# Other heaps for the down-projection's 1/rms products and for the copies and sums between seven half products

## The chip, the cores and the metric

The kernel runs on one core of a Trainium2 chip. The metric is the device time of one execution in microseconds (us). The engines of the core are named as the profile names them: PE is TensorE (matmuls), PEld its weight loads, DVE is VectorE, ACT is ScalarE, POOL is GpSimd and SP is SyncE, which issues the DMAs here.

## The reference

The input x has 512 tokens of 1,024 features. Two layers of a first block (a feed-forward network, a mixer of a recurrent scan, dilated attention and a convolution, and a second feed-forward network) are followed by a second block: a gated linear attention (GLA) mixer, a feed-forward network with a three-tap convolution on its gate, a sparse attention mixer (NSA), a second such feed-forward network, and a last RMS norm. What the change touches is the feed-forward network (FFN), six times in all, and the norms ahead of whatever comes behind one:

```python
def _rms_norm(x, g):
    xf = x.astype(jnp.float32)
    y = xf * lax.rsqrt(jnp.mean(xf * xf, axis=-1, keepdims=True) + NORM_EPS)
    return y.astype(x.dtype) * g
...
def _swiglu(x, w_gate, w_up, w_down):
    return (jax.nn.silu(x @ w_gate) * (x @ w_up)) @ w_down
```

The hidden width is 2,816, that is 22 tiles of 128.

## The kernel before

Activations lie feature by feature, 128 features on the partitions and 512 tokens in a row, so x is eight tiles of 128x512. Each float32 matrix is cut into a high part (`hi`, `whi`, by ACT) and a low part (`lo`, `wlo`, by DVE, source minus high part), and a product is three matmuls: high by high, high by low, low by high.

An FFN (`ffn`, L455) first scales x and takes the sums of squares for 1/rms (`norm_r`, L332: squares `nsq` on ACT, their sum `nacc` on POOL, a product with ones into the bank `po`); the factor R = 1/rms is multiplied in behind the products. Then it walks over the 22 hidden tiles in two halves of 11. A tile is made in one of two ways. `eight` makes gate and up by eight k-tiles each, 48 matmuls of 512 columns. `seven` splits the 2x2 product of gate and up weights by token halves in Strassen's manner (Winograd's form): seven products instead of eight, each 12 matmuls of 256 columns, summed in the halves of two PSUM banks X and Y. Products 1 and 2 go to the first half of X, 5 and 3 to the second, 6 and 7 to the first half of Y, 4 to the second. The four plain FFNs have 11 such tiles each (SEVEN, L155: 5, 6, 8, 9, 11, 12, 14, 15, 17, 18, 20, so five pairs of neighbours and a single one), the two with the convolution 8 each (SEVEN_CONV, L156: 5, 7, ... 19). That is 60.

In a `seven` tile, DVE makes sums of the weights (L403, L404 into `ws`; L408 and L410 in place into `raw`), and `cut` (L365 on ACT, L366 on DVE) splits them. The cut of L404's sum is the second half of S (products 5 and 6), the cut of L403's is the first half. L410's result is cut into `wsh` and `wsl` (W, product 3). Between products, ACT copies the halves of X to `wp` (P, L429 behind product 1, L433 behind product 5), and DVE adds: `fv` (L431 behind product 6, L438 behind product 7), `fu` (L439, L440), `fg` (L436, L442, L443). Behind each half of the hidden tiles, the down-projection makes eight output tiles by `gemm` (L280 to L282); L483 multiplies each by R into `fd`, and L484 adds it to x. The last norm is `final` (L1475): squares on ACT (L1481), sums on POOL (L1483), `po` on PE (L1487), `nms` on DVE (L1491).

SBUF tiles of 128x512 come from heaps (HEAPS, L149): a heap is a ring of slots, given out in the order of the program text: n, x, r0 and r1 have 16, aq 7, ap 6, o 3 and rs 3. A new tile of a heap takes the slot of an old one and waits until that one's last reader is through. `ws`, `wp`, `fg`, `fu`, `fv` lie in r0, `wsh` and `wsl` in ap, and `fd` in the default heap, which an FFN sets to o (`self.on("o", "rr")`); the norms' `nacc`, `nsq` and `bex` lie in o as well.

The order of each engine's instructions isn't that of the text: a list scheduler orders them by a modelled timeline and by priorities (`RANK`), and takes the slots' waits into account. So a heap's change can move instructions on every engine.

Of the kernel before, what the change touches and what calls it, by code (L numbers as in the profile page):

```python
# [18 lines left out]
T = 512  # L19
# [171 lines left out]
class Net:  # L191
# [202 lines left out]
    def seven(self, wgu, f, F, R):  # L394


        n, H = T // 2, D // 2
        a, b = slice(0, n), slice(n, T)
        p, q = slice(0, H), slice(H, D)
        rg, ru = [self.raw(wgu[f, :, i * D:(i + 1) * D], D) for i in range(2)]  # L400
        s1, s2 = [self.s([128, H], "ws", heap="r0") for _ in range(2)]
        S, G, U = self.parts(D), self.parts(D), self.parts(D)
        self.V.tensor_tensor(s1, ru[:, p], ru[:, q], OP.add)  # L403
        self.V.tensor_tensor(s2, s1, rg[:, p], OP.subtract)  # L404
        self.cut(rg, *G)
        self.cut(s2, *[t[:, q] for t in S])
        self.cut(s1, *[t[:, p] for t in S])
        self.V.tensor_tensor(ru[:, p], rg[:, p], ru[:, p], OP.subtract)  # L408
        self.cut(ru, *U)
        self.V.tensor_tensor(rg[:, q], rg[:, q], s2, OP.subtract)  # L410
        W = [self.s([128, H], nm, F32R, "ap") for nm in ("wsh", "wsl")]
        self.cut(rg[:, q], *W)
        half = lambda t, c: [y[:, c] for y in t]
        A = {1: half(G, p), 2: half(G, q), 3: W, 4: half(U, q), 5: half(S, p), 6: half(S, q), 7: half(U, p)}
        X, Y = [self.ps([128, T], next(self.banks)) for _ in range(2)]

        def product(i, ps, first=False):
            hi, lo = A[i]
            for j in range(4):
                xh, xl = F[i][j]  # L420
                w = slice(j * 128, (j + 1) * 128)
                self.T.matmul(ps, hi[:, w], xh, start=first and j == 0, stop=False, skip_group_check=True)  # L422
                self.T.matmul(ps, hi[:, w], xl, start=False, stop=False, skip_group_check=True)  # L423
                self.T.matmul(ps, lo[:, w], xh, start=False, stop=j == 3, skip_group_check=True)  # L424

        P, g, u, v = [self.s([128, T], nm, heap="r0") for nm in ("wp", "fg", "fu", "fv")]
        B, E = Y[:, a], Y[:, b]
        product(1, X[:, a], True)
        self.A.activation(P[:, a], X[:, a], AF.Copy)  # L429
        product(6, B, True)  # L430
        self.V.tensor_tensor(v[:, a], B, P[:, a], OP.add)  # L431
        product(5, X[:, b])
        self.A.activation(P[:, b], X[:, b], AF.Copy)  # L433
        product(4, E)
        product(2, X[:, a])
        self.V.tensor_tensor(g[:, a], X[:, a], R[:, a], OP.mult)  # L436
        product(7, B)
        self.V.tensor_tensor(v[:, b], B, P[:, a], OP.add)  # L438
        self.V.tensor_tensor(u[:, a], E, v[:, b], OP.add)  # L439
        self.V.tensor_tensor(u[:, b], v[:, b], P[:, b], OP.add)  # L440
        product(3, X[:, b])
        self.V.tensor_tensor(g[:, b], X[:, b], v[:, a], OP.add)  # L442
        self.V.tensor_tensor(g[:, b], g[:, b], R[:, b], OP.mult)  # L443
        return g, u

    def eight(self, wgu, f, xs, R):
# [5 lines left out]
        return g, pu  # L452

    def ffn(self, x, gname, l, wgu, wdn, scale, seven, conv=None):


        self.on("o", "rr")
        xs = self.scaled(x, gname, KT * l)
        R = self.norm_r(x)
        factors = self.seven_x(x, xs, gname, KT * l)  # L460
        F = next(factors)
        self.banks = cycle(("mm", "rr", "at", "mm", "rx", "at"))
        M = NF // 2
        for part in range(2):
            h = []
            for i in range(M):
                f = part * M + i
                g, u = self.seven(wgu, f, F, R) if f in seven else self.eight(wgu, f, xs, R)
                if conv:
                    g = conv(g, l, f)  # L470
                self.A.activation(g, g, AF.Silu)
                self.V.tensor_tensor(g, u, g, OP.mult)
                h.append(self.split(g, None, HALF[i]))
                if 1 <= f < 5:
                    next(factors)
            for n in range(KT):
                pd = self.ps([128, T], next(self.banks))
                for a, b in ((0, 6), (6, M)):
                    o = part * M
                    w = self.load_w(wdn[n, :, (o + a) * 128:(o + b) * 128], (b - a) * 128)  # L480
                    self.gemm(pd, w, h.__getitem__, a, b, a == 0, b == M)
                y = self.s([128, T], "fd")
                self.V.scalar_tensor_tensor(y, pd, scale, R, OP.mult, OP.mult)  # L483
                self.V.tensor_tensor(x[n], x[n], y, OP.add)  # L484
        self.banks = repeat("mm")
# [1121 lines left out]
```

## Time and profile before

| | us |
|---|---|
| Time, median of 3 runs | 3455.41 |
| Lowest and highest run | 3453.07, 3463.67 |
| Profiled execution, its time | 3454.09 |
| Profiled execution, its span | 3452.3 |
| PE busy | 3381.1 (98%) |
| DVE busy | 2273.9 (66%) |
| ACT busy | 1448.1 (42%) |
| POOL busy | 324.5 (9%) |
| Mean granted clock of TensorE | 0.992 |

The span runs from the first to the last instruction of the profiled execution. Matmuls are pipelined: a row of the timeline gives a matmul's start and duration, and the next starts before it has ended, so the spacing of the starts is what a matmul costs. The idle time in brackets is counted from the end of the one ahead. A granted clock of 1.00 is 2.4 GHz, one of 0.50 is 1.2 GHz.

### The profile page before, as it was taken

How to read it: one execution, taken by the hardware profiler on the slowest of the kernel's cores; microseconds unless marked ns; L12 is line 12 of the kernel's file. 1: busy time of each engine (PE TensorE's matmuls, PEld its weight loads, DVE VectorE, ACT ScalarE, POOL GpSimd, SP SyncE). 2: the span in 40 equal slices, each digit the busy share in tenths (PEclk: the TensorE clock that was granted, in tenths of full speed). 3: DMA queues.
4: the chain of work that ended last, by engine and by line, in shares of the span. 5: the costliest groups of instructions: out<-in, count | busy, mean ns of one | idle time of the engine just before them, and what ended most of it. 6: DMA issues, size and time to landing. Idle time of an engine off the chain costs nothing.

```text
span 3452.3 us, 49155 instructions
## 1 busy us (share of the span) xinstructions
PE 3381.1 (98%) x19286; PEld 2798.2 (81%) x19286; DVE 2273.9 (66%) x3973; ACT 1448.1 (42%) x2390; POOL 324.5 (9%) x377
## 2 busy tenths in 40 slices
PE   8999999999999999999999999999999999999997
PEld 7888777878888889877878888777888887788886
DVE  7566597667575757569766666486766664467573
ACT  5333434354243424343445334344533444654342
POOL 1000116010001000013301000120100010210000
PEclk9999999999999999999999999999999999999998
DMA  4333322132333232423123333321333442132322
GB/s 135 100 102 101 116 81 63 38 128 89 93 98 101 92 94 97 115 94 79 47 87 98 97 94 115 117 71 53 104 88 102 135 121 79 50 113 83 106 88 67
DMA packets 134536, 321.94 MB, mean 93 GB/s; under 512 B 33152, under 2 KB 35744, under 8 KB 134304
## 3 DMA queue, kind: packets, MB, share of 16 engines
q1 hardware_dynamic: 134304, 318.81, 30.3%
q8 instruction: 151, 2.47, 0.3%
q14 instruction: 81, 0.66, 0.1%
HBM read 303.81 MB, written 14.94 MB: 92 GB/s over the span
## 4 chain that ended last, share of the span: by engine, by line
PE 47%; DVE 4%; ACT 1%; issue 0%; POOL 0%; POOLq 0%; DVEq 0%; ACTq 0%
PE mm L280 5%; PE mm L281 5%; PE mm L282 5%; PE at L281 3%; PE at L280 3%; PE at L282 3%; PE rx L281 2%; PE rx L282 2%; PE rx L280 2%; PE rr L281 1%; PE rr L282 1%; PE rr L280 1%; PE mm L422 1%; PE mm L424 1%; PE mm L423 1%; PE at L424 1%
## 5 line engine op out<-in xcount | busy, mean ns | idle before, releaser
L268 ACT ACTIVATE whi<-raw 128x1024 fp32r<-128x1024 f32 (+3 forms) x494 | 444.2, 900 | 899.7 <-PE mm L281 363.3
L269 DVE TENSOR_TENSOR wlo<-raw,whi 128x1024 fp32r<-128x1024 f32 (+3 forms) x494 | 518.4, 1050 | 262.4 <-ACT whi L268 261.4
L280 PE MATMUL mm<-xh,whi 128*128 128x512 f32 x896 | 359.6, 402 | 8.5 <-ACT whi L268 8.4
L282 PE MATMUL mm<-xh,wlo 128*128 128x512 f32 x896 | 361.4, 403 | 0.0
L281 PE MATMUL mm<-xl,whi 128*128 128x512 f32 x896 | 359.7, 401 | 0.0
L341 POOL TENSOR_TENSOR nacc<-nacc,nsq 128x512 f32<-128x512 f32 x70 | 106.4, 1520 | 1994.3 <-ACT nsq L340 1991.5
L280 PEld LDWEIGHTS mm<-xh,whi 128*128 128x128 f32 x896 | 169.9, 190 | 52.8 <-ACT whi L268 8.4
L280 PE MATMUL mm<-hi,whi 128*128 128x512 f32 x520 | 206.0, 397 | 2.5 <-ACT hi L297 1.4
L281 PEld LDWEIGHTS mm<-xl,whi 128*128 128x128 f32 x896 | 169.6, 189 | 44.8 <-issue 6.0
L282 PE MATMUL mm<-hi,wlo 128*128 128x512 f32 x520 | 205.8, 396 | 0.0
L281 PE MATMUL mm<-lo,whi 128*128 128x512 f32 x520 | 205.6, 395 | 0.1
L282 PEld LDWEIGHTS mm<-xh,wlo 128*128 128x128 f32 x896 | 169.5, 189 | 41.4 <-issue 3.2
L281 PE MATMUL at<-xl,whi 128*128 128x512 f32 x496 | 197.2, 398 | 0.0
L282 PE MATMUL at<-xh,wlo 128*128 128x512 f32 x496 | 196.9, 397 | 0.0
L280 PE MATMUL at<-xh,whi 128*128 128x512 f32 x496 | 196.1, 395 | 0.0
L365 ACT ACTIVATE whi<-raw 128x1024 fp32r<-128x1024 f32 x120 | 127.2, 1060 | 147.6 <-PE mm L423 55.5
L366 DVE TENSOR_TENSOR wlo<-raw,whi 128x1024 fp32r<-128x1024 f32 x120 | 146.5, 1221 | 37.9 <-ACT whi L365 37.9
L422 PE MATMUL mm<-xh,whi 128*128 128x256 f32 x552 | 158.2, 287 | 4.3 <-ACT wp L429 4.1
L424 PE MATMUL mm<-xh,wlo 128*128 128x256 f32 x552 | 156.5, 283 | 0.9 <-DVE wlo L366 0.7
L281 PE MATMUL at<-lo,whi 128*128 128x512 f32 x396 | 156.8, 396 | 0.0
L282 PE MATMUL at<-hi,wlo 128*128 128x512 f32 x396 | 156.8, 396 | 0.0
L280 PE MATMUL at<-hi,whi 128*128 128x512 f32 x396 | 155.6, 393 | 0.0
(748 smaller groups left out, 8472.3 us busy)
## 6 DMA issues: line engine op xcount, KB each, us to landing
raw<-ffn_gu SPq DMA_DIRECT2D x176, 512.0 KB
raw<-c_gu SPq DMA_DIRECT2D x88, 512.0 KB
raw<-ffn_dn SPq DMA_DIRECT2D x64, 384.0 KB
raw<-w_in SPq DMA_DIRECT2D x46, 512.0 KB
raw<-ffn_dn SPq DMA_DIRECT2D x64, 320.0 KB
raw<-c_dn SPq DMA_DIRECT2D x32, 384.0 KB
raw<-c_dn SPq DMA_DIRECT2D x32, 320.0 KB
raw<-a_w_in SPq DMA_DIRECT2D x17, 512.0 KB
```

The lines of the kernel that those rows point to most:

```text
L268: self.A.activation(hi, raw, AF.Copy)
L269: self.V.tensor_tensor(lo, raw, hi.bitcast(F32), OP.subtract)
L280: self.T.matmul(ps, wh, xh, start=first and j == 0, stop=False)
L281: self.T.matmul(ps, wh, xl, start=False, stop=False)
L282: self.T.matmul(ps, wl, xh, start=False, stop=last and j == nk - 1)
L341: self.G.tensor_tensor(acc, acc, sq, OP.add)
L365: self.A.activation(hi, src, AF.Copy)
L366: self.V.tensor_tensor(lo, src, hi.bitcast(F32), OP.subtract)
L422: self.T.matmul(ps, hi[:, w], xh, start=first and j == 0, stop=False, skip_group_check=True)
L423: self.T.matmul(ps, hi[:, w], xl, start=False, stop=False, skip_group_check=True)
L424: self.T.matmul(ps, lo[:, w], xh, start=False, stop=j == 3, skip_group_check=True)
```

## The change

Three names move to the heap ap: `wp` and `fv` of `seven` from r0, and `fd` of the down-projection from o. `fg` and `fu` stay in r0. The counts of instructions on each engine stay. The added line moves every line behind L426 by one: L429 becomes L430.

```diff
@@ -423,7 +423,8 @@
-        P, g, u, v = [self.s([128, T], nm, heap="r0") for nm in ("wp", "fg", "fu", "fv")]
+        P, v = [self.s([128, T], nm, heap="ap") for nm in ("wp", "fv")]
+        g, u = [self.s([128, T], nm, heap="r0") for nm in ("fg", "fu")]
...
@@ -479,7 +480,7 @@
-                y = self.s([128, T], "fd")
+                y = self.s([128, T], "fd", heap="ap")
```

The text of one engine's work is moved by the scheduler. ACT in the second tile of a pair of neighbours (the tile at 237 to 252 us of the trace), before; `whi_2149` is S, `whi_2153` U, and `at_2171` and `mm_2172` are the banks X and Y:

```order
L429 ACTIVATE wp_2173<-at_2171 128x256
L365 ACTIVATE whi_2149<-ws_2148 128x512
L365 ACTIVATE whi_2153<-raw_2145 128x1024
L365 ACTIVATE wsh_2167<-raw_2143 128x512
L433 ACTIVATE wp_2173<-at_2171 128x256
L471 ACTIVATE fg_2041<-fg_2041 128x512
```

The same place now:

```order
L365 ACTIVATE whi_2149<-ws_2148 128x512
L365 ACTIVATE whi_2153<-raw_2145 128x1024
L365 ACTIVATE wsh_2167<-raw_2143 128x512
L430 ACTIVATE wp_2173<-at_2171 128x256
L472 ACTIVATE fg_2042<-fg_2042 128x512
```

The first copy to `wp` has moved from ahead of S's second half to behind `wsh`. PE in the same tile, before, from the end of the tile ahead (`wsh_2034`, product 3) on; the next five rows but one belong to products 5 (bank `at_2171`) and 6 (bank `mm_2172`):

```order
L424 MATMUL mm_2038<-xh_148,wsl_2035 128x256
L422 MATMUL at_2171<-xh_341,whi_2149 128x256
L423 MATMUL at_2171<-xl_342,whi_2149 128x256
L422 MATMUL mm_2172<-xh_345,whi_2149 128x256
L423 MATMUL mm_2172<-xl_346,whi_2149 128x256
L424 MATMUL at_2171<-xh_341,wlo_2150 128x256
L422 MATMUL at_2171<-xh_428,whi_2149 128x256
```

The same place now, with the start of product 5 and of product 4 (`whi_2153`) behind the lines left out:

```order
L424 MATMUL mm_2038<-xh_148,wsl_2035 128x256
L422 MATMUL mm_2172<-xh_345,whi_2149 128x256
L423 MATMUL mm_2172<-xl_346,whi_2149 128x256
L424 MATMUL mm_2172<-xh_345,wlo_2150 128x256
L422 MATMUL mm_2172<-xh_432,whi_2149 128x256
...
L424 MATMUL mm_2172<-xh_606,wlo_2150 128x256
L422 MATMUL at_2171<-xh_341,whi_2149 128x256
...
L424 MATMUL at_2171<-xh_602,wlo_2150 128x256
L422 MATMUL mm_2172<-xh_345,whi_2153 128x256
```

Product 6 now runs whole ahead of product 5, and product 4 follows at once. ACT at the end of the program, in the last down-projection, before (`x` is the residual, `vec` holds the norm's weights):

```order
L268 ACTIVATE whi_30762<-raw_30760 128x640
L1481 ACTIVATE nacc_30784<-x_27082 128x512
L1481 ACTIVATE nsq_30788<-x_27084 128x512
L1489 ACTIVATE x_27082<-x_27082,vec 128x512
L1489 ACTIVATE x_27084<-x_27084,vec 128x512
L1481 ACTIVATE nsq_30792<-x_27086 128x512
```

And now:

```order
L268 ACTIVATE whi_30493<-raw_30491 128x768
L1482 ACTIVATE nacc_30784<-x_27082 128x512
L1490 ACTIVATE x_27082<-x_27082,vec 128x512
L268 ACTIVATE whi_30517<-raw_30515 128x640
L268 ACTIVATE whi_30542<-raw_30540 128x768
L1482 ACTIVATE nsq_30788<-x_27084 128x512
L1490 ACTIVATE x_27084<-x_27084,vec 128x512
L268 ACTIVATE whi_30566<-raw_30564 128x640
```

The squares and the scaling of the last norm stood behind the last weight cut (`whi_30762`); now those of the first six tiles of x stand between the cuts, and those of the last two behind them.

## Rows read from the trace of the kernel before

**Rows 1.** The page, busy time of each engine, with its share and instructions:

```profile
PE 3381.1 (98%) x19286; PEld 2798.2 (81%) x19286; DVE 2273.9 (66%) x3973; ACT 1448.1 (42%) x2390; POOL 324.5 (9%) x377
```

**Rows 2.** PE's waits: line waited for, us in total, times, longest us:

```profile
PE po L1487 <- POOL nacc L1483: 9.0, 1, 9.0
PE rx L422 <- ACT wp L429: 5.1, 10, 1.5
```

**Rows 3.** Timeline of DVE, a pair's second tile: start, us, operation, [idle before]:

```profile
239.34 0.43 DVE L436 TENSOR_TENSOR fg<-mm,bR 128x256 f32<-128x256 f32 x1 [1.32 <-PE mm L424]
240.34 0.68 DVE L403 TENSOR_TENSOR ws<-raw 128x512 f32<-128x512 f32 x1
241.06 0.69 DVE L404 TENSOR_TENSOR ws<-ws,raw 128x512 f32<-128x512 f32 x1
243.81 0.68 DVE L366 TENSOR_TENSOR wlo<-ws,whi 128x512 fp32r<-128x512 f32 x1
247.09 0.42 DVE L431 TENSOR_TENSOR fv<-mm,wp 128x256 f32<-128x256 f32 x1
```

**Rows 4.** Timeline of ACT in the same tile:

```profile
241.68 0.37 ACT L429 ACTIVATE wp<-at 128x256 f32<-128x256 f32 x1
241.94 0.62 ACT L365 ACTIVATE whi<-ws 128x512 fp32r<-128x512 f32 x1
243.92 0.63 ACT L365 ACTIVATE wsh<-raw 128x512 fp32r<-128x512 f32 x1 [0.41 <-DVE raw L410]
```

**Rows 5.** Timeline of PE in the same tile:

```profile
242.10 0.38 PE L422 MATMUL at<-xh,whi 128*128 128x256 f32 x1 [0.24 <-ACT wp L429]
245.72 0.28 PE L424 MATMUL mm<-xh,wlo 128*128 128x256 f32 x1
```

**Rows 6.** Timeline, PE and DVE, first pair of the first FFN:

```profile
71.95 0.39 PE L422 MATMUL rx<-xh,whi 128*128 128x256 f32 x1 [0.24 <-ACT wp L429]
72.13 0.68 DVE L366 TENSOR_TENSOR wlo<-ws,whi 128x512 fp32r<-128x512 f32 x1
82.52 0.39 PE L422 MATMUL mm<-xh,whi 128*128 128x256 f32 x1 [0.47 <-ACT wp L429]
```

**Rows 7.** Timeline, PE and DVE, a tile of a convolution FFN:

```profile
2532.35 0.28 PE L424 MATMUL mm<-xh,wlo 128*128 128x256 f32 x1
2532.24 0.69 DVE L366 TENSOR_TENSOR wlo<-ws,whi 128x512 fp32r<-128x512 f32 x1
2536.45 0.42 DVE L431 TENSOR_TENSOR fv<-rr,wp 128x256 f32<-128x256 f32 x1
```

**Rows 8.** Timeline, PE and DVE, first seven-product tile of a convolution FFN:

```profile
2488.89 0.39 PE L422 MATMUL rx<-xh,whi 128*128 128x256 f32 x1 [1.55 <-ACT wp L429]
2490.77 0.68 DVE L366 TENSOR_TENSOR wlo<-ws,whi 128x512 fp32r<-128x512 f32 x1
```

**Rows 9.** Windows, PE: stretch, us, busy (matmuls), granted clock, DMA share, GB/s:

```profile
2489.40:2492.80 3.40, 3.00 (x22) 1.00 0.00 0
3120.40:3123.80 3.40, 3.40 (x17) 0.50 0.06 14
244.40:247.80 3.40, 3.40 (x29) 1.00 0.23 35
```

**Rows 10.** Timeline of ACT, POOL, PE and DVE at the last norm:

```profile
3428.70 1.15 ACT L1481 ACTIVATE nsq<-x 128x512 f32<-128x512 f32 x2 [5.84 <-DVE x L484]
3429.47 6.65 POOL L1483 TENSOR_TENSOR nacc<-nacc,nsq 128x512 f32<-128x512 f32 x5 [6.41 <-ACT nsq L1481]
3437.90 1.84 PE L1487 MATMUL po<-cpack,nsq 128*128 128x1 f32 x8
3439.78 0.16 DVE L1491 TENSOR_SCALAR nms<-po 128x4 f32<-128x4 f32 x1 [11.12 <-PE po L1487]
```

**Rows 11.** Timeline of POOL and PE at the norm ahead of GLA:

```profile
2206.89 11.08 POOL L341 TENSOR_TENSOR nacc<-nacc,nsq 128x512 f32<-128x512 f32 x7 [363.03 <-ACT nsq L340]
2227.03 1.08 PE L324 MATMUL po<-cpack,bex 128*128 128x128 f32 x4 [3.85 <-DVE bex L321]
```

## The prediction

> **What bounds the kernel now.** I read the page's busy times first: TensorE is busy 98% of the span [rows 1], so every microsecond that it doesn't wait is taken, and the time can only move where it waits now or will wait. The profiled execution took 3454.1 us (span 3452.3 and 1.8 around it), which stands in the middle of the runs' 3453.1 to 3463.7, 1.3 under their median; I sum against it. Next I read TensorE's waits: the largest is one of 9.0 us for the sum of squares before the last norm, and the next kinds are short repeated ones of the seven-product tiles for the copy `wp` [rows 2]. Then I read the timelines of VectorE, ScalarE and TensorE in one such tile, the second of a pair at 237 to 252 us, which repeats 16 times [rows 3, 4, 5], and the rows of the other kinds of tile.
>
> In that tile product 1's part ends and the next matmul would start at 241.70 (the row at 242.10 waited 0.24, and matmuls here start 0.16 before the one ahead has ended). It starts at 242.10, when `wp` (241.68 + 0.37 = 242.05) is there; 24 matmuls later the last of products 5 and 6 starts at 245.72 instead of 241.70 + 23 x 0.12 = 244.46 [rows 5]. The tile costs 1.25 us of waiting. The 0.12 us is the spacing at full clock: 29 matmuls in 3.40 us [rows 9]. What holds the tile is VectorE: it works without a gap from 239.34 (waiting for TensorE's product 2) through L440, L403, L404, the cuts, to L431 at 247.09 [rows 3].
>
> **Part 1: `wp` and `fv` in heap ap.** No instruction is added or removed; only orders change. In ap the slots are handed out in program order, and `wsh` and `wsl` stand ahead of `wp` there; ScalarE so writes `wp` behind `wsh` (order excerpt of ScalarE), whose input L410 comes late: `wsh` starts at 243.92 and ends at 244.55 [rows 4], while `wp` was done at 242.05. TensorE's program pays for it: product 5, which needs `wp` read out of its bank, no longer opens with two matmuls beside two of product 6; all twelve of 6 come first, then 5, then 4 at once (order excerpt of TensorE).
>
> *Second tile of a pair, 16 times.* (i) Product 6 needs `whi`'s second half, cut from L404's result (241.06 + 0.69 = 241.75 [rows 3]); with `wp` gone from ahead of it the 0.62 us cut [rows 4] ends near 242.46, so the first matmul starts at 242.51 in place of 241.70: 0.81, and 0.10 for the slow first step that follows each pause (0.22 to the next one, not 0.12). (ii) The third matmul of product 6 needs the second half of `wlo`, which VectorE finishes at 243.81 + 0.68 = 244.49 [rows 3]; VectorE's order is the same up to there in both programs. TensorE would be there at 242.85 and starts at 244.54: 1.69 + 0.10. Before, ten matmuls of product 5 covered this wait. (iii) Product 4 writes the bank that L431 reads, and L431 ends at 247.09 + 0.42 = 247.51 [rows 3]; product 4 is reached 10 + 12 matmuls on, at 247.28, and starts at 247.55: 0.27 + 0.10. Before, product 2 covered it. Sum 3.07 for 1.25: +1.82 x 16 = **+29.1**.
>
> *First pair of the four plain FFNs, 4 times.* First tile: `wp` cost 0.24 + 0.16 + 0.10 = 0.50; now the third matmul of product 6, due at 71.55, waits for the cut that ends at 72.81 [rows 6]: 72.86 - 71.55 = 1.31 + 0.10 = 1.41, +0.91. Second tile: it waits 0.23 longer than the other pairs' at its start (0.47 against 0.24 [rows 5, 6]), so about 1.5, and gets the order above, 3.07: +1.57. Together +2.5 x 4 = **+10**.
>
> *Tiles of the two convolution FFNs.* In ten of them product 1 ends at 2532.35 [rows 7] and the like; the third matmul of 6, due 0.36 later at 2532.71, waits for `wlo` (2532.24 + 0.69 = 2532.93), starts at 2532.98: 0.27 + 0.10. Product 5 follows, and product 4, due at 2535.72, waits for L431 (2536.45 + 0.42 = 2536.87 [rows 7]): 1.20 + 0.10. Less the 0.49 for `wp` that goes, +1.18 in the six tiles of this order; in four tiles two matmuls of 512 columns (0.47) stand between 5 and 4, so +0.71. 6 x 1.18 + 4 x 0.71 = +9.9. The first tile of each FFN waits 1.55 for `wp` and 2.7 in all its pauses now; by [rows 8] product 6's third matmul, due at 2488.89 - 1.55 + 0.08 = 2487.42, starts behind 2490.77 + 0.68 = 2491.45: 4.08 + 0.10, +1.5 each. Together **+12.9**.
>
> **Part 2: `fd` out of heap o.** Heap o has three slots and is then left to the norm's squares and sums; they need not wait behind the last `fd`. At the end, five additions of 6.65 us on GpSimd and 16 small matmuls run after the last sum of x, and `nms` starts at 3439.78 [rows 10]. In the new program the squares of six of the eight tiles stand between the cuts of the last down-projection (order excerpt of ScalarE at the end), and the seventh follows its sum; only the last tile's square is left, starting at 3428.70 (two take 1.15), then 8 matmuls (1.84, or half at full clock [rows 10]): `nms` at 3430.3 to 3431.3, a gain of 8.5 to 9.4; **-9.0**. The norm ahead of the GLA mixer is the same case: seven additions of 11.08 us run after 2206.89, and TensorE waits 3.85 us for the broadcast at 2227.03 [rows 11]: **-3.9**, as a later wait there stays. What hides the squares now is the down-projection, where ScalarE and GpSimd have room; the 7 squares of 0.6 us add to ScalarE before the weight cuts, bounded by 0 and by one square (0.6) for each of 6 FFNs; I take 0. The order in the mixers shifts too; TensorE shows no wait for a norm there, so between -5 and +5, taken as 0.
>
> **The clock.** With these alone: 3454.1 + 29.1 + 10 + 12.9 - 9.0 - 3.9 = 3493. The pause of 1.55 us and the shorter ones behind it at 2488 were followed by a granted clock of 1.00 (2.4 GHz) [rows 8, 9]; the same tile of the second convolution FFN, with the same pauses, was followed from 3120 by 3.4 us at 0.50 (1.2 GHz), 17 matmuls where 29 fit [rows 9], and so was the old 1.25 us of pauses at 242 [rows 9]. A fall costs 12 matmuls of 0.12, about 1.5 us, less the 0.3 of product 4's wait that it swallows: 1.2. The new pauses are 2.6 to 3.1 us, in 20 pairs. One of two cases fell, so I take half: 10 x 1.2 = **+12**. Forecast: 3505 us. By the Trainium skill, TensorE: Matmul & The Clock Gate, section "A second HAM failure mode: psum-queue depth-cycling", an engine that idles briefly between groups of matmuls can swing between its two clocks again and again. The trace agrees at one of the two spots, 0.50 at 3120 and 1.00 at 2489; by the page all pairs would fall, rival B.
>
> **Rivals.** *A: no pair loses the clock.* The stalls come as worked out, 3493 us. For it: 1.00 behind the pauses at 2488; against: 0.50 at 3120.
>
> *B: every pair and both long tiles lose it.* 22 x 1.5 = 33 on 3493: 3526 us. For it: the new pauses together are longer than those that did it once.
>
> *C, the other side: the heap r0 was what held the cuts.* A seven-product tile takes six of r0's 16 slots now and four afterwards. If `ws` (L403) could then start earlier, both halves of `wlo` would be ready when product 6 comes. It decides at L403 about 1.8 us earlier: from there the second tile costs no more than now, and the time is 3454.1 - 12.9 = 3441; with 3 us more, all waits go, 16 x 1.25 + 4 x 2.0 in pairs and 10 x 0.5 + 2 x 2.7 in the convolution FFNs: 28 + 10 more, 3403 us. Against it: L403 starts at 240.34, back to back with the VectorE work ahead of it, which is held by TensorE's product 2 (1.32 us of idle before 239.34), not by a slot [rows 3], and in the new order it stands in the same place. The Trainium skill, Perfetto Trace Analysis, section "Identifying Performance Opportunities", says that a gap that repeats on the engine that should be saturated can mean that memory for the next tile was lacking. That would be this rival and its 3441 or less; the trace disagrees, since the gap's cause is VectorE's queue without idle time.
>
> *D: it moves nothing that counts.* If the stalls grew by only a quarter of my sum, 13 us, the 12.9 of part 2 would eat it: 3454 us. It would need ScalarE's `wp` ahead of L410 after all, which the program's order excludes.
>
> **How the numbers follow.** Forecast with half of the clock losses, 3505: 0.48. A, 3493: 0.22. B, 3526: 0.18. C: 0.06. D: 0.06. The predicted time is 3505. The low end, 3482, takes A with 11 us for the unknowns (mixers 5, one wait of part 1 mis-sized by 0.3 us in 20 pairs); the high end, 3528, takes in B. About 0.3%, 10 us, can be told from no change by a measurement here. Slower by more than that: forecast, A and B, 0.88; the same 0.06 (D); faster 0.06 (C).
>
> **What would show it.** In the changed profile TensorE's waits in the seven-product tiles should be for L366's `wlo` (about 1.6 us, 20 times) and no longer for `wp`; a pair's second tile should show three waits near 0.8, 1.7 and 0.3 us; the row of `wsh` ahead of `wp` on ScalarE; the 9.0 us wait before `po` gone and `nms` under 2 us after the last square; the 3.85 us at the GLA norm gone. The granted clock behind the pairs tells the forecast from A and B: half of them at 0.50. It would be wrong if L403 started earlier against product 1's end (C), or if waits that I took as covered, the weight cuts of the eight-product tile behind a pair, came out late.

## The result, and the profile after

The changed kernel takes 3505.48 us (median of 4 runs, 3503.80 to 3505.86) against 3458.36 us of the kernel before (3453.07 to 3463.67): the ratio is 1.0135, with a 95% interval of 1.0117 to 1.0153. The change makes the kernel slower by 1.35%. The forecast was 3505 us, in a range of 3482 to 3528. The profiled execution took 3505.73 us, with a span of 3503.9, which is 51.6 more than that of before; by the medians the change costs 47.1 us.

The page of the changed kernel, busy time of each engine:

```profile
PE 3390.4 (97%) x19286; PEld 2813.0 (80%) x19286; DVE 2256.9 (64%) x3973; ACT 1448.3 (41%) x2390; POOL 317.8 (9%) x377
```

The counts of instructions are those of [rows 1]; PE's share fell from 98% to 97% while the span grew by 51.6 us, so most of the loss is waiting, on the engine that has no time to give. PE's busy time grew too, by 9.3 us (3381.1 to 3390.4) for the same matmuls; the clock below accounts for it in part. PE's waits (line waited for, us in total, times, longest) say on what:

```profile
PE mm L424 <- DVE wlo L366: 18.9, 12, 1.6
PE rr L424 <- DVE wlo L366: 12.6, 8, 1.6
...
PE mm L422 <- ACT whi L365: 7.2, 12, 0.6
PE at L424 <- DVE wlo L366: 7.1, 6, 1.2
PE rr L422 <- ACT whi L365: 4.9, 8, 0.6
PE at L422 <- ACT whi L365: 4.8, 2, 2.4
PE at L422 <- DVE fv L432: 4.1, 4, 1.0
...
PE po L1488 <- ACT nsq L1482: 1.4, 1, 1.4
```

No row for `wp` is left among them, where it led before [rows 2]. In its place stand 12 + 8 = 20 waits of up to 1.6 us for the second half of `wlo`, as many as there are pairs, 20 of 0.6 us for `whi`, and some for L432 (L431 before). The wait of 9.0 us before `po` has shrunk to 1.4 us.

The timeline of the pair whose old rows are [rows 3 to 5], now at 246 to 256 us (start, us, operation, [idle before]). PE:

```profile
250.68 0.39 PE L422 MATMUL mm<-xh,whi 128*128 128x256 f32 x1 [0.61 <-ACT whi L365]
252.76 0.39 PE L424 MATMUL mm<-xh,wlo 128*128 128x256 f32 x1 [1.57 <-DVE wlo L366]
```

DVE at the same place:

```profile
247.55 0.42 DVE L437 TENSOR_TENSOR fg<-mm,bR 128x256 f32<-128x256 f32 x1 [1.32 <-PE mm L424]
...
248.22 0.41 DVE L441 TENSOR_TENSOR fu<-fv,wp 128x256 f32<-128x256 f32 x1
248.55 0.68 DVE L403 TENSOR_TENSOR ws<-raw 128x512 f32<-128x512 f32 x1
...
251.41 0.69 DVE L410 TENSOR_TENSOR raw<-raw,ws 128x512 f32<-128x512 f32 x1
252.02 0.69 DVE L366 TENSOR_TENSOR wlo<-ws,whi 128x512 fp32r<-128x512 f32 x1
...
255.29 0.42 DVE L432 TENSOR_TENSOR fv<-mm,wp 128x256 f32<-128x256 f32 x1
```

DVE does the same work in the same order at the same pace: from its wait for product 2 to the end of the second cut pass 252.71 - 247.55 = 5.16 us, as before (244.49 - 239.34 = 5.15 [rows 3]). What changed is what PE has to do meanwhile: it has put product 6 first and has nothing else until that cut lands at 252.71; it goes on at 252.76.

The end of the program, ACT:

```profile
3489.63 0.63 ACT L1482 ACTIVATE nsq<-x 128x512 f32<-128x512 f32 x1 [6.31 <-DVE x L485]
```

and DVE:

```profile
3491.41 0.16 DVE L1492 TENSOR_SCALAR nms<-po 128x4 f32<-128x4 f32 x1 [1.86 <-PE po L1488]
```

From the first square behind the last sum of x to `nms` are 1.78 us, where 11.08 us passed before [rows 10]. Now it is the only one left; before, the squares of six tiles still had to be made there.

### The profile page after: what moved, and what is told of

Same layout as the page of the kernel before. It is cut to its first block, busy times and chain, and to the rows that moved or that the text cites. A ratio compares the mean times of both kernels' runs of the same rounds, so it can differ in the third digit from the quotient of the medians.

```text
span 3503.9 us, 49159 instructions
## 1 busy us (share of the span) xinstructions
PE 3390.4 (97%) x19286; PEld 2813.0 (80%) x19286; DVE 2256.9 (64%) x3973; ACT 1448.3 (41%) x2390; POOL 317.8 (9%) x377
## 4 chain that ended last, share of the span: by engine, by line
PE 86%; DVE 10%; issue 1%; POOL 1%; ACT 1%; DMA 0%; SPq 0%; DVEq 0%; POOLq 0%; ACTq 0%
PE mm L282 9%; PE mm L281 9%; PE mm L280 9%; PE at L282 6%; PE at L280 6%; PE at L281 6%; PE rx L280 3%; PE rx L282 3%; PE rx L281 3%; PE rr L282 2%; PE rr L280 2%; PE mm L422 2%; PE rr L281 2%; PE mm L424 2%; PE mm L423 2%; DVE wlo L366 2%
## 5 line engine op out<-in xcount | busy, mean ns | idle before, releaser
L269 DVE TENSOR_TENSOR wlo<-raw,whi 128x1024 fp32r<-128x1024 f32 (+3 forms) x494 | 510.1, 1034 | 308.4 <-ACT whi L268 307.2
L424 PE MATMUL mm<-xh,wlo 128*128 128x256 f32 x552 | 159.1, 288 | 19.1 <-DVE wlo L366 18.9
L422 PE MATMUL mm<-xh,whi 128*128 128x256 f32 x552 | 160.5, 291 | 10.0 <-ACT whi L365 7.2
L366 DVE TENSOR_TENSOR wlo<-raw,whi 128x1024 fp32r<-128x1024 f32 x120 | 146.6, 1221 | 36.5 <-ACT whi L365 36.5
L423 PE MATMUL mm<-xl,whi 128*128 128x256 f32 x552 | 158.0, 286 | 0.0
```

The costliest lines, as they stand in the source:

```text
L269: self.V.tensor_tensor(lo, raw, hi.bitcast(F32), OP.subtract)
L366: self.V.tensor_tensor(lo, src, hi.bitcast(F32), OP.subtract)
```

## The experiments

Each kernel is the one named with the edit shown. Times are medians of the runs, with the kernel before measured on the same chip beside them (3459.5 us for the first four, 3460.2 for the next four, 3460.4 for the last three).

**1. `fd` alone.** The kernel before with:

```diff
-                y = self.s([128, T], "fd")
+                y = self.s([128, T], "fd", heap="ap")
```

> The kernel before with fd alone moved to heap ap. My theory: the products' order in the seven-product tiles stays that of before, and the gains at the two norms come alone: the 9 us wait at the last norm and the 3.9 to 8 us at the GLA norm go, so 3454 - 13 to 17 = 3437 to 3441 us, and TensorE's waits for wp stay as they were (about 12.5 us in all). Rival (fd crowds the six slots of ap and it is that which delays wp): the pairs show the 1.6 us waits for wlo, and the time is above 3490 us.

Measured: 3442.6 us (3435.0 to 3446.7), ratio 0.995 (0.9938 to 0.9963). The order of the products stays, and PE's waits are those of before without the one of 9.0 us (`rx` for `wp` 5.4 us in 10 waits, `mm` 3.8, `at` 3.4). So `fd` in ap is the whole of the gain and none of the loss. The 16.9 us are the expected 13 to 17; the time stands above the expected 3437 to 3441 because the kernel before took 3459.5 us here and not 3454.

**2. `wp` and `fv` alone.** The kernel before with the first half of the diff only:

```diff
-        P, g, u, v = [self.s([128, T], nm, heap="r0") for nm in ("wp", "fg", "fu", "fv")]
+        P, v = [self.s([128, T], nm, heap="ap") for nm in ("wp", "fv")]
+        g, u = [self.s([128, T], nm, heap="r0") for nm in ("fg", "fu")]
```

> The kernel before with wp and fv moved to heap ap, fd left in o. My theory: all of the loss and none of the gain: 3454 + 52 of waits + about 12 of lost clock = 3518 us, with the 9 us wait at the last norm still there. Rival (the loss needs all three names in ap): near 3454. For the clock: the pauses are the same as in the changed kernel but lie at other times; if the same pairs lose the clock (9 of 20 there), it depends on what stands around the pair, if others do, on when the pause falls.

Measured: 3526.2 us (3521.3 to 3526.6), ratio 1.0188 (1.0174 to 1.0202). All of the loss is here, 67 us, where 64 had been put (52 and 12). PE's waits:

```profile
PE mm L424 <- DVE wlo L366: 18.9, 12, 1.6
PE rr L424 <- DVE wlo L366: 12.6, 8, 1.6
PE po L1488 <- POOL nacc L1484: 9.0, 1, 9.0
```

The first two rows are to the tenth those of the changed kernel, and the 9.0 us before the last norm are back. 8 of the 20 pairs were followed by a half-speed stretch, and 6 of these 8 are not among the 9 of the changed kernel.

**3. The cut of `wsh` behind the copy to `wp`.** The changed kernel, with all three names in ap, and one line moved in the text:

```diff
-        self.cut(rg[:, q], *W)
...
         self.A.activation(P[:, a], X[:, a], AF.Copy)
+        self.cut(rg[:, q], *W)
```

> The changed kernel, all three names in ap, with one line moved in the program text: the cut into wsh and wsl is written behind the first copy to wp instead of ahead of it. My theory (slots of a heap are handed out in the order in which the text first writes their tiles, so wp waited for the cut of wsh): wp comes early again, products 5 and 6 are again interleaved, the waits of 1.6 us for wlo go, and the time is that of before less the gains at the norms, 3437 to 3441 us, perhaps 5 less since wp may come ahead of both halves of whi. Rival (ap has too few slots for five names): 3505 us as the changed kernel.

Measured: 3432.6 us (3428.3 to 3438.5), ratio 0.9924 (0.9912 to 0.9937). ACT in the same tile of a pair:

```profile
241.51 0.38 ACT L430 ACTIVATE wp<-at 128x256 f32<-128x256 f32 x1 [4.50 <-PE at L424]
242.17 1.30 ACT L365 ACTIVATE whi<-ws 128x512 fp32r<-128x512 f32 x2 [0.27 <-DVE ws L403]
243.44 1.06 ACT L365 ACTIVATE whi<-raw 128x1024 fp32r<-128x1024 f32 x1
244.97 0.63 ACT L365 ACTIVATE wsh<-raw 128x512 fp32r<-128x512 f32 x1 [0.48 <-DVE raw L410]
```

`wp` stands ahead of everything again, products 5 and 6 are interleaved, and PE's waits in this tile are 0.16 us for `whi` and 0.37 us for `wlo`, not 0.61 and 1.57. Five names share the six slots as in the changed kernel, so the heap isn't too small: the order in which the text first writes `wsh` and `wp` makes the difference. With another order `wp` also gets another slot, so a slot that was still in use could have been the reason. The first seven-product tile of the changed kernel speaks against it: nothing has been written in ap before, all six slots are free, and ACT still has `wp` behind `wsh`:

```profile
73.44 0.63 ACT L365 ACTIVATE wsh<-raw 128x512 fp32r<-128x512 f32 x1 [0.17 <-DVE raw L410]
73.98 0.37 ACT L430 ACTIVATE wp<-rx 128x256 f32<-128x256 f32 x1
```

A pair's second tile waits as long here as before the change. That the kernel is faster than those of experiments 1 and 4 does not come from the pairs: the plain FFNs take 308.5 to 308.9 us each in all three, and the first two mixers together take some 15 us less here.

**4. `wp` back in r0.** The changed kernel with `fv` and `fd` in ap, `wp` in r0:

```diff
-        P, v = [self.s([128, T], nm, heap="ap") for nm in ("wp", "fv")]
-        g, u = [self.s([128, T], nm, heap="r0") for nm in ("fg", "fu")]
+        P, g, u = [self.s([128, T], nm, heap="r0") for nm in ("wp", "fg", "fu")]
+        v = self.s([128, T], "fv", heap="ap")
```

> The changed kernel with wp alone put back into r0; fv and fd stay in ap. My theory: only wp stands behind wsh in a way that costs, so the order of products is that of before and the time is 3437 to 3441 us. Rival (fv in ap costs as well): up to 20 us more, with TensorE waiting for L432 before product 4.

Measured: 3438.1 us (3436.5 to 3442.8), ratio 0.9944 (0.9931 to 0.9956). As experiment 1 within the spread: `fv` in ap costs nothing, `wp` there costs all.

**5. The tile of `wp` asked for first.** The changed kernel with:

```diff
-        W = [self.s([128, H], nm, F32R, "ap") for nm in ("wsh", "wsl")]
+        P = self.s([128, T], "wp", heap="ap")
+        W = [self.s([128, H], nm, F32R, "ap") for nm in ("wsh", "wsl")]
...
-        P, v = [self.s([128, T], nm, heap="ap") for nm in ("wp", "fv")]
+        v = self.s([128, T], "fv", heap="ap")
```

> The changed kernel with the tile of wp asked for ahead of the tiles wsh and wsl in the text; the order of the instructions in the text is that of the change. Theory as the prediction put it (slots go by the order in which the text asks for the tiles): wp comes early again and the time falls to 3437 to 3441 us. Theory as sharpened by the run with the later cut (slots go by the order in which the text first writes the tiles): nothing changes, 3505 us with the 1.6 us waits for wlo.

Measured: 3507.6 us in one run, with the waits for `wlo` of the changed kernel (18.9 and 12.6 us). So, with experiment 3, it isn't where the text asks for a tile that counts, but where it first writes it; the prediction had the former.

**6. The sums L403 and L404 on GpSimd, in the changed kernel.**

```diff
-        self.V.tensor_tensor(s1, ru[:, p], ru[:, q], OP.add)
-        self.V.tensor_tensor(s2, s1, rg[:, p], OP.subtract)
+        self.G.tensor_tensor(s1, ru[:, p], ru[:, q], OP.add)
+        self.G.tensor_tensor(s2, s1, rg[:, p], OP.subtract)
```

> The changed kernel with the two sums of weights L403 and L404 on GpSimd in place of VectorE, so that they need not stand behind L440. The order 6, 5, 4 of the products stays. My theory (the pair's three waits come from VectorE's queue, which brings both halves of S late): the waits of 0.8 and 1.7 us in the pairs vanish and most of those in the convolution tiles, and with them the lost clock: 20 x 2.5 + 10 + 12 = some 70 us less, 3425 to 3445 us, unless GpSimd's two sums (about 1.3 us each) are themselves late. Rival (the order of the products alone costs, whoever brings the data): near 3505 us.

Measured: 3498.3 us (3496.0 to 3501.1), ratio 1.0109 (1.0092 to 1.0126): a miss, near the rival's figure, but not for the rival's reason. PE and DVE in the second tile of a pair:

```profile
250.88 0.39 PE L424 MATMUL mm<-xh,wlo 128*128 128x256 f32 x1 [1.82 <-DVE wlo L366]
```

```profile
247.90 0.69 DVE L366 TENSOR_TENSOR wlo<-ws,whi 128x512 fp32r<-128x512 f32 x1
248.86 0.42 DVE L443 TENSOR_TENSOR fg<-mm,fv 128x256 f32<-128x256 f32 x1 [0.28 <-PE mm L424]
249.21 0.68 DVE L410 TENSOR_TENSOR raw<-raw,ws 128x512 f32<-128x512 f32 x1
249.80 0.42 DVE L444 TENSOR_TENSOR fg<-fg,bR 128x256 f32<-128x256 f32 x1
250.14 0.69 DVE L366 TENSOR_TENSOR wlo<-ws,whi 128x512 fp32r<-128x512 f32 x1
```

Both halves of `whi` now come early, and the 0.6 us wait for them is gone, as the theory has it. But the second cut of `wlo` did not come forward as much. L443 still stands ahead of it and now waits for PE's product 3, and the scheduler has put L444 ahead of it too. That cut ends at 250.83, 4.53 us behind L437 (246.30) instead of 5.16; but PE, no longer held by `whi`, is there 0.8 us earlier too, and waits 1.82 us for it where it waited 1.57. The wait for L432 is gone as well. So a pair gained about 1.0 us where the clock held, by its period from first tile to first tile (33.44 us here, 34.42 in the changed kernel; see the pairs below):

```profile
203.71 0.28 PE L422 MATMUL mm<-xh,whi 128*128 128x256 f32 x1
237.15 0.28 PE L422 MATMUL mm<-xh,whi 128*128 128x256 f32 x1
```

Inside the six FFNs the profiled execution is 17.3 us shorter than that of the changed kernel, where some 70 had been put: 9 pairs still lose the clock. And 16.4 us of it are lost again in the second mixer, which the edit does not touch and which has 30.7 us at half speed here, against 6.8. The releaser is still DVE's cut, so the rival (order alone, whoever brings the data) isn't borne out either; the run shows that work taken off a queue need not bring forward what waits in it, and that a whole kernel's time can hide a gain in its FFNs.

**7. The same two sums on GpSimd in the kernel of experiment 3.**

> The kernel with the later cut (3433 us) with L403 and L404 on GpSimd. If VectorE's queue is what makes a pair's second tile wait before the change too (1.25 us each, and 0.5 to 2.7 us in the convolution tiles), 20 to 35 us go: 3400 to 3412 us. Rival (wp or GpSimd's pace sets those waits): 3425 to 3435 us. GpSimd sharing the memory port with VectorE would show as longer VectorE operations.

Measured: 3417.8 us (3413.8 to 3419.6), ratio 0.9877 (0.9862 to 0.9892), the fastest of all, 1.2% ahead of the kernel before, but a miss: 15 us less than experiment 3, where 20 to 35 had been put, and outside the rival's range as well. In the second tile of a pair PE's longest wait left is

```profile
243.99 0.39 PE L424 MATMUL mm<-xh,wlo 128*128 128x256 f32 x1 [0.18 <-DVE wlo L366]
```

The pair's period is 32.08 us, 0.54 less than in experiment 3 (32.62), not the 1.25 expected, and the first pair of each plain FFN has a wait of 1.6 us for `wlo`. The releaser of both waits is still DVE's cut.

**8. The changed kernel once more, unaltered.**

> The changed kernel once more, unaltered. In the profiled execution 9 of 20 pairs and both first convolution tiles lost the clock. If the loss is set by the program's own work, the same 9 pairs lose it again; if by the moment at which the chip looks, another set does, in about the same number, and the time stays within some 5 us of 3505.

Measured: 3512.4 us, one run, 7 us above 3505 where 5 had been allowed; 5.1 us of it are in the first mixer, with 30.7 us at half speed there against 23.9. 8 pairs lost the clock, all of them among the 9 of the first profile; the ninth, at 253 us, did not. The windows of that pair (stretch, us, PE busy and matmuls, granted clock, DMA share, GB/s), first profile with a pair before it that kept the clock:

```profile
218.90:222.30 3.40, 3.29 (x28) 1.00 0.41 92
253.30:256.70 3.40, 3.40 (x21) 0.60 0.42 105
```

and in the second:

```profile
253.30:256.70 3.40, 3.29 (x27) 1.00 0.53 151
```

So neither of the two expectations holds alone: the set is nearly the program's own, and one pair went the other way. Experiment 5, with the same waits of PE, agrees: 7 pairs fell there, all among the same 9.

**9. L410 alone on GpSimd, in the changed kernel.**

```diff
-        self.V.tensor_tensor(rg[:, q], rg[:, q], s2, OP.subtract)
+        self.G.tensor_tensor(rg[:, q], rg[:, q], s2, OP.subtract)
```

> The changed kernel with L410 alone on GpSimd. On VectorE nothing else moves; L410 stands there between the two halves of S's low part, 0.60 us of its queue. My theory (product 6's third matmul waits for VectorE's queue): the wait for the second half of wlo falls from 1.6 to 1.0 us in all 20 pairs, so 12 us less there, and some us less in the convolution tiles: 3485 to 3494 us. Rival (something else, such as the change of banks or TensorE's own order, sets the pause): 1.6 us as before and 3505 us. If GpSimd's L410 (about 1.3 us) made wsh and so wp late, a new wait of product 5 for L430 would show.

Measured: 3503.2 us (3502.4 to 3506.8), ratio 1.0127 (1.0112 to 1.0142). The wait did not fall, by the rows of the same pair on PE, POOL and DVE:

```profile
252.19 0.39 PE L424 MATMUL mm<-xh,wlo 128*128 128x256 f32 x1 [1.72 <-DVE wlo L366]
```

```profile
249.47 1.52 POOL L410 TENSOR_TENSOR raw<-raw,ws 128x512 f32<-128x512 f32 x1 [14.86 <-ACT whi L365]
```

```profile
250.11 2.03 DVE L366 TENSOR_TENSOR wlo<-ws,whi 128x512 fp32r<-128x512 f32 x2
```

The two cuts of `wlo` stand back to back now, and should take 0.60 + 0.68 = 1.28 us; they take 2.03. The grouped rows of L366 (min, median and max ns of one) of the changed kernel and of this one:

```profile
L366 DVE TENSOR_TENSOR wlo<-ws,whi x120: 678/684/693, 72.1 to 3393.4; 128x512 fp32r<-128x512 f32 x120
```

```profile
L366 DVE TENSOR_TENSOR wlo<-ws,whi x120: 675/680/1766, 71.0 to 3390.8; 128x512 fp32r<-128x512 f32 x120
```

The first of the two runs into GpSimd's L410 (249.47 to 250.99) and ends only after it. The 0.60 us that left the queue came back as 0.75 us of DVE standing still. The releaser and DVE's unbroken run of work say that the queue sets the wait, as the theory has it, but this run does not prove it: the step taken away was given back. The time says less still. In the profiled execution the FFNs took 9 us more than in the changed kernel, and the first mixer, with 3.4 us at half speed in place of 23.9, 13 us less.

**10 and 11. L408, and L410, on GpSimd too, in the kernel of experiment 7.**

> The kernel with the later cut and L403 and L404 on GpSimd (3418 us), with L408 on GpSimd too. VectorE's queue between product 2 and the second half of S is 0.6 us shorter, so if it still sets what is left of the pairs' waits, 3405 to 3415 us; if GpSimd's three sums in a row (some 4.5 us) are late, 3418 to 3430 us.

Measured: 3418.8 us (3417.6 to 3422.7), no gain on 3417.8 and the figure of the second case. A pair's period is 32.33 us for 32.08. The longest cut of `wlo` from `ws` was 1782 ns there, against a median of 685, which points to the same holding up as in experiment 9; that this is the cause was not tested.

> The kernel with the later cut and L403 and L404 on GpSimd (3418 us), with L410 on GpSimd too, which stands between the two halves of S's low part on VectorE. By VectorE's queue 0.6 us less in 20 pairs: 3404 to 3412 us; if wsh gets late for product 3 instead, 3418 or more.

Measured: 3432.3 us (3431.2 to 3437.7), slower, and a miss. The plain pairs' second tile is 0.4 us shorter there (period 31.67 us for 32.08), as expected, so the loss is elsewhere: the granted clock was at half speed for 66 us in all against 28 us in experiment 7, and the difference lies in the two mixers (44.4 us against 6.8), which took 24.5 us more. Why the mixers lose more clock in one build than in another was not tried.

## Why the prediction was right

Stage by stage, after less before, profiled executions, us. An FFN's stage runs from the start of the first matmul of its first seven-product tile to the start of its last `fd`:

| Stage | measured | forecast |
|---|---|---|
| start to the first tile | +1.2 | 0 |
| four plain FFNs, inside | +12.84, +12.85, +11.82, +10.75 = +48.3 | 29.1 + 10 = 39.1, and clock |
| two convolution FFNs, inside | +8.8, +7.2 = +16.0 | 12.9, and clock |
| first and second mixer | +6.0, -2.2 | -5 to +5 each way |
| GLA mixer with its norm | -8.0 | -3.9 |
| NSA mixer | -0.4 | 0 |
| last norm to the end | -9.3 | -9.0 |
| sum | +51.6 | 39.1 + 12.9 - 3.9 - 9.0 = 39.1, and 12 for the clock: 51.1 |

That the time came out at 3505 to the microsecond is in part luck. The sum starts from the profiled 3454.1 us, and the median of the kernel before was 3458.4 us in the end; by the medians the change costs 47.1 us where 51.1 had been put. And terms that were left out cancel: the first two mixers, put at 0, cost 3.8 us (the first one 6.0, more than the 5 allowed), and the GLA norm gave 4.1 us more than forecast. The mechanism was right all the same, as its parts show.

*The pairs.* Forecast were waits near 0.8, 1.7 and 0.3 us; the first two idle times read 0.61 and 1.57 us (with the 0.16 us overlap of matmuls 0.77 and 1.73), and where the clock held, product 4's first matmul started 0.27 us late. A pair's period, from the first matmul of its first tile to that of the next pair's, was 230.19 - 197.59 = 32.60 us before:

```profile
197.59 0.28 PE L422 MATMUL mm<-xh,whi 128*128 128x256 f32 x1
230.19 0.28 PE L422 MATMUL mm<-xh,whi 128*128 128x256 f32 x1
```

and is 238.39 - 203.97 = 34.42 us in the changed kernel where the clock held:

```profile
203.97 0.28 PE L422 MATMUL mm<-xh,whi 128*128 128x256 f32 x1
238.39 0.28 PE L422 MATMUL mm<-xh,whi 128*128 128x256 f32 x1
273.93 0.28 PE L422 MATMUL mm<-xh,whi 128*128 128x256 f32 x1
```

That is 1.82 us more, the forecast's figure.

*The clock.* The second period there, 273.93 - 238.39 = 35.54 us, had the fall of the windows above: 1.12 us more, where the forecast had 1.2. 9 of the 20 pairs fell, and both long tiles of the convolution FFNs; one of these two fell before the change as well [rows 9]. The plain FFNs' 48.3 are the 39.1 of waits and 9 x 1.1 = 10. That the new pauses bring the falls is shown: in the kernel before and in experiments 1, 3 and 4, which have the old order, no pair of the plain FFNs is followed by half speed; in the six profiles with the new order 7 to 10 of the 20 are. That it would be half of them was a guess from one spot on each side, the largest uncertain term, and its coming true is luck. The prediction's clause that the old pauses at 242 us were followed by 0.50 is wrong as it reads: its own row has 1.00 there [rows 9].

*The convolution FFNs.* The sum was nearly right, its parts not all. Of the 16.0 us, some 1.6 are the one fall more (8.8 in the FFN that fell only after the change, 7.2 in the one that fell before too), so 14.4 stand against 12.9. In each first tile the pauses add up to the forecast's 4.2 us, but as 2.4 us of idle for `whi` and 1.2 for `wlo`, not as one wait. In six of the ten other tiles the two waits came as worked out. In four, product 4 stands behind two matmuls of the next tile, and these waited 1.1 us for their own weight cut:

```profile
PE at L280 <- ACT whi L268: 2.2, 2, 1.1
PE rx L280 <- ACT whi L268: 2.2, 2, 1.1
```

I had counted the two matmuls as cover, not as something that waits; the wait for `wlo` that I had put there did not come, so the tile's cost is near the forecast by two errors that cancel. Two more tiles waited for L432, which the forecast didn't have (`PE rr L422 <- DVE fv L432: 0.8, 2, 0.4`).

*The norms.* The last one gained 9.3 us as forecast. At GLA the gain was 8.0 for 3.9: beside the idle 3.85 us [rows 11] most of the stretch of low clock behind it went too (10.2 us of half speed there before, 3.4 after), a term that I left out of the sum.

*The step that was wrong though nothing hung on it.* "In ap the slots are handed out in program order, and `wsh` and `wsl` stand ahead of `wp` there" holds for the order of the first writes, not of the requests, by experiments 3 and 5. The order of the built program, which the forecast went by, was the same either way.

Of the rivals, A (no fall) and B (all fall) are excluded by the profile, with 9 of 20. The time alone would not do it as surely: 3493 and 3526 lie 12 and 21 us off, and the runs spread over 2 us, but the first mixer alone, on which the forecast put nothing, moved by 6 us. C is excluded by L403's place, directly behind L441 as it stood behind L440 before, and D by the 20 waits. That r0 has room to spare now brought nothing: experiment 1, with `wp` and `fv` in r0, is faster.

## What to carry to other kernels

Where a scheduler orders the work and a heap hands out its slots in the order of first writes, two names in one heap are tied to one another: an early, small copy whose first write stands behind that of a late tile of the same heap waited for it here, though all slots were free. When an engine is 98% busy, ask of each pair of products which of them covers the arrival of the other's data; the same instructions in another order cost 1.8 us more a pair here, and 2.9 where the clock fell. Try the halves of such a change apart: one half was worth -17 us, the other +67. And read such a change by its stages: the first two mixers took from 415 us with little or no half speed to 434 us with 30.7 us of it in these kernels, so a gain of some us in the FFNs can vanish in the whole time (experiment 6).

## What the runs showed of the hardware

An elementwise operation on GpSimd can hold one on VectorE until it has ended: a cut of 0.68 us that started at 250.11 took 1.43 us, to 251.54, beside a GpSimd operation of 1.52 us that ended at 250.99 (experiment 9). The two VectorE operations ahead of it, L408 (begun before GpSimd's) and L443 (with one source in PSUM), kept their usual 0.68 and 0.41 us. The Trainium skill, SBUF — State Buffer, section "SBUF: two separate sides", has the two engines share one pair of memory ports by an exclusive lock, not by splitting the bandwidth; the row agrees with it, since the cut ends 0.55 us behind GpSimd's operation; at half speed beside it, it would have ended some 0.2 us behind, by an estimate from the same rows.

The loss of clock behind like pauses is nearly a property of the program: 8 of 9 pairs fell again when the same kernel was run again, and 7 of them in experiment 5, while a kernel with the same pauses at other times lost it behind another set of like size (8 of 20, two of them in common). And it is not small outside the FFNs: the first mixer, with the same instructions, took 6 us more in the changed kernel, which has 13.7 us more of half speed there. What sets the clock in the mixers was not tried.
